# Diagonal blocks through memory at one stride, and two first sums placed behind the triangular steps, in a conformer and RWKV-7 trunk

## The chip, the cores and the metric

The kernel runs on one core of a Trainium2 chip. The metric is the device time of one execution in microseconds (us); smaller is better. All arithmetic is in 32-bit floating point; a product of large matrices is made of three matmuls on values split into a high and a low part (`xh·w_hi + xl·w_hi + xh·w_lo`).

## The reference

The program computes a decoder trunk of two layers on 512 tokens with 16 learned tokens ahead of them (528 in all), width 1024. A layer is a feed-forward half step, a token mixer and a second half step, each with a residual and a layer norm:

```python
h = _layer_norm(ALPHA * h + 0.5 * _swiglu(h, ffn1...), ...)
m = _mixer(h, ...)            # below
h = _layer_norm(ALPHA * h + m, ...)
h = _layer_norm(ALPHA * h + 0.5 * _swiglu(h, ffn2...), ...)

def _mixer(x, ...):
    z = x @ w_in
    glu_a, glu_b, zr, gate_c, gate_r = jnp.split(z, ...)
    yc = _conv_branch(glu_a, glu_b, ...)    # GLU, depthwise convolution of 31 taps, norm, silu, product
    yr = _rwkv_branch(zr, ...)              # 16 heads of 64
    return (sigmoid(gate_c) * yc + sigmoid(gate_r) * yr) @ w_out

def step(S, inp):                           # the recurrence of _rwkv_branch, per head, over tokens
    r_t, w_t, k_t, v_t, kk_t, a_t = inp
    sa = jnp.einsum("bhvk,bhk->bhv", S, -kk_t)
    S = S * w_t[:, :, None, :] + sa[..., None] * (kk_t * a_t)[:, :, None, :] \
        + v_t[..., None] * k_t[:, :, None, :]
    return S, jnp.einsum("bhvk,bhk->bhv", S, r_t)
```

After the recurrence each head's output gets a norm of its own (group norm), a bonus term and a gate.

## The kernel before, in words

The recurrence is computed in chunks: the 16 learned tokens, then eight chunks c = 0 to 7 of 64 tokens. Inside a chunk the steps are coupled by a lower triangular matrix of 64 x 64 for each head, which has to be inverted; between chunks only a 64 x 64 state is handed on. The 16 heads are worked through in four groups q = 0 to 3 of four heads. Of a group, these stages matter here:

- **Scores** (`scores`, L1354): for each chunk eight small matmuls on TensorE (PE) form the coupling matrix. ScalarE (ACT) copies it to `ut` (L1359), VectorE (DVE) masks the other parts (L1361, L1363), and SyncE (SP) writes it to a buffer in memory, `mscr<-ut` (L1366).
- **Substitution** (`substitution(q, g)`; g = 0 for chunks 0 to 3, g = 1 for chunks 4 to 7): a 64 x 64 matrix has four diagonal blocks of 16 x 16. They are loaded from memory so that each of 64 partitions holds one block, `im<-mscr` (L1380), inverted by 30 short DVE steps, the triangular steps (L1389 and L1392, `is<-im,ix` and `ix<-ix,is`), copied transposed by ACT (`it`, L1396), written to memory, `xdscr<-ix` and `xdscr<-it` (L1398), and read back into `dd`, `dd<-xdscr` (L1403), where the blocks stand on the diagonal of a 64 x 64 matrix whose other elements are zero. `dd` has two halves, f = 0 (from `ix`) and f = 1 (from `it`).
- **Inverse** (`inverse(q, g)`): PE completes the inverse of the whole matrices, first with half f = 0 (L1428), then with f = 1 (L1435), with a DVE operation after each step.
- **Scan**: chunk after chunk PE, ACT and DVE carry the state through (L1510, L1512, L1523, L1526, L1532, L1539). The inverse for g = 0 must be there before chunk 0, that for g = 1 before chunk 4.
- **Post**: group norm (`group_norm`; its first sum is `reduce_sum` at L1570, later `b<-b,gn_st` at L1585), bonus and gate of an earlier part, while the next group is under way.

The scan of one group overlaps scores and substitution of the next. At the last group, q = 3, there is no next group; there the convolution's norm begins: loads `G<-cscr` (L945) and seven additions on DVE over eight 128 x 528 pieces (L948, `conv_mean`), a sum over partitions on PE (L935), and `conv_norm` (L956 onward). The 31 taps of the convolution (L1183, `cacc`) run on DVE all through the mixer.

What keeps PE busy during these chains is a list of large products that don't depend on them: the gates' and GLU's share of `x @ w_in` (L250, matmuls of 128 x 264, below called fillers). They are handed out between the steps.

Each engine works in order. That order is chosen when the kernel is built, by a list scheduler with estimated durations of its own; it takes what is ready by its estimate, and obeys the dependences and order constraints without a semaphore (`nosync`), such as those between the triangular steps. So a change of a duration or of a constraint in one place may reorder all engines in the mixers.

Of the kernel before, what the change touches and what calls it, by code (L numbers as in the profile page):

```python
# [11 lines left out]
ALU = mybir.AluOpType  # L12
AX = mybir.AxisListType
# [3 lines left out]
P = 128  # L17
# [3 lines left out]
NM = 16  # L21
# [8 lines left out]
HS = 64  # L30
C = 64
NCH = SEQ // C
LN_EPS = 1e-5
GN_EPS = 64e-5
ALPHA = (2 * DEPTH) ** 0.25
# [72 lines left out]
class Trunk:  # L108
# [686 lines left out]
    def mixer(self, l, last, pre, more):  # L795
        nc, tc = self.nc, self.tc
        self.l, self.last = l, last
        self.t0, self.n = (NM, SEQ // 2) if last else (0, T // 2)
        dram = lambda name, shape: self.dp.tile(shape, F32, name=f"{name}{l}")
# [3 lines left out]
        self.gs = dram("gscr", [2 * D, T])  # L803
        self.us = dram("uscr", [D, T])
        self.ds, self.as_, self.ggs = dram("dscr", [D, T]), dram("ascr", [D, T]), dram("ggscr", [D, T])
        self.ms = dram("mscr", [4, NCH * 4, C, C])
        self.ms0 = dram("mscr0", [4, 4, NM, NM])
        self.xs0 = dram("xscr0", [4, 4, NM, NM])
        self.xd = dram("xdscr", [4, 2, 2, P // 2, NM, NM])
        ppool, self.pp = self.enter(f"mix_ps{l}", space=PSUM)  # L810
        pms = [self.mm() for _ in range(2)]
        self.glu0 = self.sc()
# [55 lines left out]
        N = prep(1)  # L868
        post = iter(())
        self.cuts = CUTS  # L870
        for q in range(4):
# [3 lines left out]
            for c, _ in enumerate(self.scan(q, Q)):  # L875
                if c == 0:
                    if q == 3:
                        self.tap_late = 150
                        self.taps(KT * TAPS)
                        cv = self.conv_mean()  # L880
# [58 lines left out]
    def conv_mean(self):  # L939
        nc, mp, t0, n = self.nc, self.mp, self.t0, self.n  # L940
        s = slice(t0, t0 + 2 * n)
        cv = self.rows().rearrange("p a b c t -> p (a b c) t")[:, :, s]
        csv = self.cs.rearrange("(o p) t -> p o t", p=P)
        for a, b in zip(CV, CV[1:]):
            nc.sync.dma_start(out=cv[:, a:b], in_=csv[:, a:b, s])  # L945
        ssum, mean = (mp.tile([P, T], F32, name="v", bufs=4)[:, 0:2 * n] for _ in range(2))
        for o in range(1, KT):
            nc.vector.tensor_tensor(ssum, cv[:, 0] if o == 1 else ssum, cv[:, o], op=ALU.add)  # L948
        nc.scalar.copy(mean.rearrange("p (h t) -> p h t", h=2), self.over_partitions(ssum))
        return cv, ssum, mean  # L950

# [110 lines left out]
    def mixer_begin(self, zs, filler):  # L1062
# [4 lines left out]
        z = self.tmp()  # L1067
# [72 lines left out]
            o += n  # L1140

        self.dd = mp.tile([P, NCH * 2, 2, C], F32, name="dd")
        nc.gpsimd.memset(self.dd, 0.0)


    def glu_b(self, ct):
# [162 lines left out]
    def scores(self, q, Q):  # L1309
# [30 lines left out]
        for c in range(NCH):  # L1340
            cs = slice(NM + c * C, NM + (c + 1) * C)
            fs = slice(2 * cs.start, 2 * cs.stop)
            ps = self.sc()
            for p in range(2):
                nc.tensor.transpose(ps[:, 0, 256 + p * P:256 + (p + 1) * P], FB[p][:, fs],
                                    self.ident)
            nc.scalar.copy(SB[:, c, :, C:2 * C],
                           ps[:, 0, 256:512].rearrange("p (h v) -> p h v", h=4))
            U = self.ut[C * (c % 2):C * (c % 2) + C, 4 * (c // 2):4 * (c // 2) + 4, :]
            pairs = []  # L1350
            for p in range(2):
                for e in range(2):
                    r = slice(HS * e, HS * e + HS)
                    pairs.append(nc.tensor.matmul(ps[:, e, p * P:(p + 1) * P], FB[p][r, fs],  # L1354
                                                  G[r, p, 1, :, cs], start=True, stop=True))
            for later, earlier in zip(pairs[1:], pairs):
                self.nosync(later, earlier)
            pv = ps[:, :, 0:2 * P].rearrange("a e (p f t) -> a e p f t", p=2, f=2)
            nc.scalar.copy(U.rearrange("a (p e) t -> a e p t", e=2), pv[C:P, :, :, 0, :])  # L1359
            mask = self.msk[:, :, None, None].to_broadcast([P, 2, 2, 2, C])  # L1360
            nc.vector.tensor_tensor(SB[:, c, :, 0:C].rearrange("a (p e) t -> a e p t", e=2),  # L1361
                                    pv[:, :, :, 1, :], mask[:, 1], op=ALU.mult)
            nc.vector.tensor_tensor(G[0:C, :, :, 0, cs].rearrange("a p e t -> a e p t"),  # L1363
                                    pv[0:C, :, :, 0, :], mask[0:C, 0], op=ALU.mult)
            to = 4 * (4 * (c // 4) + 2 * (c % 2) + c % 4 // 2)
            nc.sync.dma_start(out=self.ms[q, to:to + 4].rearrange("h j t -> j h t"), in_=U)  # L1366
            yield

    def substitution(self, q, g, Q):


        nc, mp, dd = self.nc, self.mp, self.dd
        N = NCH * 2
        blocks = [slice(NM * b, NM * b + NM) for b in range(4)]
        np_ = 4 * N + (4 if g == 0 else 0)
        M, X, XT = (mp.tile([P, NM, NM], F32, name=x, bufs=2)[0:np_] for x in ("im", "ix", "it"))
        nc.gpsimd.memset(X, 0.0)
        nc.gpsimd.memset(X.rearrange("s t i -> s (t i)")[:, 0::NM + 1], 1.0)
        for b, r in enumerate(blocks):
            nc.sync.dma_start(out=M[b * N:(b + 1) * N], in_=self.ms[q, g * N:(g + 1) * N, r, r])  # L1380
        if g == 0:
            nc.sync.dma_start(out=M[4 * N:], in_=self.ms0[q])
        steps = []
        for j in range(NM - 1):
            w, k = NM - 1 - j, j + 1
            y = mp.tile([P, 64], F32, name="is", bufs=2)[0:np_, 0:w * k]
            y = y.rearrange("s (t i) -> s t i", t=w)
            x = X[:, j + 1:, 0:k]
            steps.append(nc.vector.tensor_tensor(  # L1389
                y, M[:, j, j + 1:, None].to_broadcast([np_, w, k]),  # L1390
                X[:, j, None, 0:k].to_broadcast([np_, w, k]), op=ALU.mult))
            steps.append(nc.vector.tensor_tensor(x, x, y, op=ALU.add))  # L1392
        for later, earlier in zip(steps[1:], steps):
            self.nosync(later, earlier)
        self.hold = steps[-1]
        nc.scalar.copy(XT, X.rearrange("s t i -> s i t"))  # L1396
        for f, x in enumerate((X, XT)):
            nc.sync.dma_start(out=self.xd[q, g, f], in_=x[0:4 * N])  # L1398
            for b, r in enumerate(blocks):
                for e in range(2):  # L1400
                    o = C * e + NM * b
                    k = b * N + e * N // 2
                    nc.sync.dma_start(out=dd[o:o + NM, g * N // 2:(g + 1) * N // 2, f, r],  # L1403
                                      in_=self.xd[q, g, f, k:k + N // 2]
                                      .rearrange("s t i -> t s i"))
        if g == 0:
            nc.sync.dma_start(out=self.xs0[q], in_=XT[4 * N:])
            xt0 = mp.tile([P, 64], F32, name="xt", bufs=1)[0:NM].rearrange("a (s t) -> a s t", s=4)
            nc.sync.dma_start(out=xt0, in_=self.xs0[q].rearrange("s i t -> i s t"))
            Q["xt0"] = xt0  # L1410
# [150 lines left out]
    def group_norm(self, y, np_, m):  # L1561
# [5 lines left out]
        sq = mp.tile([P, NCH * 4, 32], F32, name="b4", bufs=B4)  # L1567
        sq = sq.rearrange("p a b -> p (a b)").rearrange("p (g v) -> p g v", v=HS)
        sb = st[:np_, :g, None].to_broadcast([np_, g, HS])
        nc.vector.reduce_sum(st[:np_, :g], yv, axis=AX.X)  # L1570
        if m in GNACT:
            mu = mp.tile([P, 16], F32, name="gn_mu", bufs=2)
            nc.vector.tensor_scalar_mul(mu, st, -1.0 / HS)
# [238 lines left out]
```

## Time and profile before

| | |
|---|---|
| time before, median of 3 runs (lowest to highest) | 3013.95 us (3011.65 to 3015.38) |
| the profiled execution: its time, its span | 3008.79 us, 3007.1 us |
| mean granted TensorE clock over the span | 0.994 |
| busy: PE, DVE, ACT, POOL | 2936.7, 2272.8, 1417.0, 181.4 us |
| TensorE not busy | 70.4 us |

The span runs from the first to the last instruction on the core. "PE" is TensorE's matmuls, "PEld" its weight loads, "SPq" a queue's own instructions on SyncE, which issue transfers. A wait is printed as engine, written tile and line, then what it waited for; then us in total, number of times, longest. The granted clock is 1.00 at full speed.

### The profile page before, as it was taken

What the parts mean: (1) busy time and instruction counts of PE and PEld (TensorE: products, weight loads), DVE (VectorE), ACT (ScalarE), POOL (GpSimd) and SP (SyncE); (2) the same over time, 40 slices, a digit from 0 to 9 for tenths busy, and PEclk for the clock granted to TensorE, in tenths of its full rate; (3) what the DMA queues carried; (4) which work ended last, traced back from release to release, by engine and by line L of the source; (5) the groups of instructions that cost most, each with busy time, mean ns of one, the idle gap of its engine ahead of it and who ended that gap; (6) DMA issues with size and microseconds to landing.
All of it is one profiled execution on the core that took longest, in us unless ns stands there. A gap on an engine that the chain in (4) does not pass through costs nothing. (4 is left out here: it accounts for less than half of the span.)

```text
span 3007.1 us, 64793 instructions
## 1 busy us (share of the span) xinstructions
PE 2936.7 (98%) x26420; PEld 2809.8 (93%) x26420; DVE 2272.8 (76%) x4657; ACT 1417.0 (47%) x2513; POOL 181.4 (6%) x288
## 2 busy tenths in 40 slices
PE   9999999999999999999999999999999989999998
PEld 8999989888888999999999999898888879999998
DVE  5776778998887768676776767789888777677767
ACT  4444444354555534444444444543444564355543
POOL 1110000000000000100001000000000000001100
PEclk9999999999999999999999999999999999999999
DMA  7565534435455645565555654444354656456651
GB/s 193 139 158 129 130 108 154 109 100 128 107 151 140 186 141 131 136 149 127 130 131 137 148 134 123 132 143 106 90 132 104 169 139 194 125 142 147 149 145 56
DMA packets 556152, 405.33 MB, mean 135 GB/s; under 512 B 89306, under 2 KB 500798, under 8 KB 555854
## 3 DMA queue, kind: packets, MB, share of 16 engines
q1 hardware_dynamic: 520302, 308.49, 36.0%
q0 software_dynamic: 30944, 84.18, 15.2%
q10 hardware_dynamic: 4608, 8.52, 0.8%
q8 instruction: 208, 3.41, 0.5%
q14 instruction: 90, 0.74, 0.1%
HBM read 270.81 MB, written 47.12 MB: 106 GB/s over the span
## 5 line engine op out<-in xcount | busy, mean ns | idle before, releaser
L218 PE MATMUL mm<-xh,w_hi 128*128 128x264 f32 (+1 forms) x1792 | 509.3, 286 | 13.0 <-ACT xh L463 8.7
L218 PE MATMUL mm<-xl,w_hi 128*128 128x264 f32 (+1 forms) x1792 | 509.4, 285 | 0.6 <-DVE xl L464 0.3
L218 PE MATMUL mm<-xh,w_lo 128*128 128x264 f32 (+1 forms) x1792 | 508.3, 284 | 0.0
L218 PE MATMUL mm<-hh,w_hi 128*128 128x264 f32 (+1 forms) x1408 | 399.6, 284 | 2.5 <-ACT hh L121 2.5
L218 PE MATMUL mm<-hh,w_lo 128*128 128x264 f32 (+1 forms) x1408 | 399.7, 284 | 0.0
L218 PE MATMUL mm<-hl,w_hi 128*128 128x264 f32 (+1 forms) x1408 | 399.3, 284 | 0.2
L250 PE MATMUL mm<-xh,w_hi 128*128 128x264 f32 x1760 | 387.2, 295 | 4.8 <-DVE tmp L1056 1.9
L250 PE MATMUL mm<-xl,w_hi 128*128 128x264 f32 x1760 | 379.8, 293 | 0.0
L1183 DVE SCALAR_TENSOR_TENSOR cacc<-cu,cw,cacc 128x528 f32<-128x528 f32 (+1 forms) x480 | 356.7, 753 | 3.6
L218 PEld LDWEIGHTS mm<-xh,w_hi 128*128 128x128 f32 x1792 | 336.6, 189 | 17.9 <-ACT xh L463 11.7
L218 PEld LDWEIGHTS mm<-xl,w_hi 128*128 128x128 f32 x1792 | 339.2, 189 | 2.9 <-DVE xl L464 2.4
L218 PEld LDWEIGHTS mm<-xh,w_lo 128*128 128x128 f32 x1792 | 338.8, 189 | 0.1
L131 ACT CAST w_hi<-sums 128x512 fp32r<-128x512 f32 (+1 forms) x204 | 154.6, 759 | 313.0 <-PE mm L218 201.7
L250 PEld LDWEIGHTS mm<-xh,w_hi 128*128 128x128 f32 x1760 | 279.4, 190 | 14.9 <-DVE tmp L1056 2.3
L250 PEld LDWEIGHTS mm<-xl,w_hi 128*128 128x128 f32 x1760 | 278.1, 190 | 7.2 <-issue 0.2
L218 PEld LDWEIGHTS mm<-hh,w_hi 128*128 128x128 f32 x1408 | 264.7, 188 | 3.1 <-ACT hh L121 2.9
L218 PEld LDWEIGHTS mm<-hl,w_hi 128*128 128x128 f32 x1408 | 264.9, 188 | 0.9 <-DVE hl L122 0.8
L218 PEld LDWEIGHTS mm<-hh,w_lo 128*128 128x128 f32 x1408 | 265.4, 189 | 0.1
L250 PE MATMUL mm<-xh,w_lo 128*128 128x264 f32 x1760 | 262.1, 292 | 0.0
L155 ACT CAST w_hi<-w_raw 128x1024 fp32r<-128x1024 f32 x130 | 136.2, 1050 | 257.3 <-PE mm L218 77.6
L164 DVE TENSOR_TENSOR w_lo<-w_raw,w_hi 128x1024 fp32r<-128x1024 f32 (+1 forms) x194 | 201.5, 1042 | 64.2 <-ACT w_hi L155 60.3
L250 PEld LDWEIGHTS mm<-xh,w_lo 128*128 128x128 f32 x1760 | 229.6, 189 | 6.4
(375 smaller groups left out, 6672.0 us busy)
## 6 DMA issues: line engine op xcount, KB each, us to landing
w_raw<-in_w_in_dram SPq DMA_DIRECT2D x116, 512.0 KB
w_lo<-w_raw POOLq DMA_DIRECT2D x100, 512.0 KB, 5.1
w_raw<-in_ffn_wg_dram SPq DMA_DIRECT2D x88, 512.0 KB
w_raw<-in_ffn_wu_dram SPq DMA_DIRECT2D x88, 512.0 KB
w_raw<-in_ffn_wd_dram SPq DMA_DIRECT2D x80, 512.0 KB
w_lo<-w_raw POOLq DMA_DIRECT2D x68, 256.0 KB, 3.6
w_raw<-in_conv_wo_dram SPq DMA_DIRECT2D x16, 512.0 KB
w_raw<-in_rwkv_wo_dram SPq DMA_DIRECT2D x16, 512.0 KB
```

The source lines that it names most:

```text
L131: self.nc.scalar.copy(hi, x)
L155: copy = self.nc.scalar.copy(hi[:, :kt], raw[:, :kt])
L164: sub = self.nc.vector.tensor_tensor(lo[:, k], raw[:, k], hi[:, k].bitcast(F32), op=ALU.subtract)
L218: self.issued = self.nc.tensor.matmul(pm, a[:, k, :], b[:, xk + k, s], start=first and k == 0 and j == 0, stop=last and k == nk - 1 and j ...
L250: m = self.issued = self.nc.tensor.matmul(pm[:, h, :n], a[:, wk + k, :], b[:, xk + k, s:s + n], start=first and i == 0, stop=last and i == ...
L1183: tap = nc.vector.scalar_tensor_tensor(y, x, w, y, op0=ALU.mult, op1=ALU.add)
```

## The change

- Each row of `mscr` (one 64 x 64 matrix) gets 64 words of room behind it, so that a row has 4160 = 4 x 1040 words. The diagonal blocks start 16 x 64 + 16 = 1040 words apart, so all 16 x 16 blocks of all rows lie at one stride. `im<-mscr` becomes one transfer of 64 x 16 x 16 elements in place of four of 16 x 16 x 16.
- `xdscr` becomes one buffer for both layers and all groups, with rows of 4160 words, zeroed once in layer 0 by two transfers of 512 KB on GpSimd's queue. `xdscr<-ix` and `xdscr<-it` write the blocks to their places on the diagonals: 1024 pieces of 64 bytes each, where they were 64 rows of 1 KB. `dd<-xdscr` then reads whole 64 x 64 matrices, zeros included: four transfers of 64 x 8 x 64 (two for each half f, pieces of 256 bytes) in place of sixteen of 16 x 8 x 16 (pieces of 64 bytes).
- `dd` is set to zero by GpSimd (L1143) in layer 0 alone.
- The first sum of group norm (L1570) and the additions of `conv_mean` (L948) get a `nosync` constraint: they come, in DVE's order, behind the last triangular step that has been put into the program so far (`self.solved`).

```diff
+DIAG = NM * (C + 1)
...
-        self.ms = dram("mscr", [4, NCH * 4, C, C])
+        self.ms = dram("mscr", [4, NCH * 4, 4 * DIAG])
...
-        self.xd = dram("xdscr", [4, 2, 2, P // 2, NM, NM])
+        if l == 0:
+            self.xd = dram("xdscr", [2, 2, NCH * 2, 4 * DIAG])
...
         for o in range(1, KT):
-            nc.vector.tensor_tensor(ssum, cv[:, 0] if o == 1 else ssum, cv[:, o], op=ALU.add)
+            add = nc.vector.tensor_tensor(ssum, cv[:, 0] if o == 1 else ssum, cv[:, o],
+                                          op=ALU.add)
+            self.nosync(add, self.solved)
...
-        nc.gpsimd.memset(self.dd, 0.0)
+        if self.l == 0:
+            nc.gpsimd.memset(self.dd, 0.0)
+            zero = self.dd.rearrange("p s f i -> p (s f i)")
+            xd = self.xd.rearrange("g f r z -> (g f r) z")
+            for a in range(2):
+                nc.gpsimd.dma_start(out=xd[:, a * C * C // 2:(a + 1) * C * C // 2],
+                                    in_=zero[a * C:(a + 1) * C])
...
+    def diagonal(x):
+
+        x = x.rearrange("r (b z) -> (r b) z", b=4)[:, 0:NM * C]
+        return x.rearrange("p (t i) -> p t i", i=C)[:, :, 0:NM]
...
-        for b, r in enumerate(blocks):
-            nc.sync.dma_start(out=M[b * N:(b + 1) * N], in_=self.ms[q, g * N:(g + 1) * N, r, r])
+        nc.sync.dma_start(out=M[0:4 * N], in_=self.diagonal(self.ms[q, g * N:(g + 1) * N]))
...
-        self.hold = steps[-1]
+        self.hold = self.solved = steps[-1]
         nc.scalar.copy(XT, X.rearrange("s t i -> s i t"))
         for f, x in enumerate((X, XT)):
-            nc.sync.dma_start(out=self.xd[q, g, f], in_=x[0:4 * N])
-            for b, r in enumerate(blocks):
-                for e in range(2):
-                    o = C * e + NM * b
-                    k = b * N + e * N // 2
-                    nc.sync.dma_start(out=dd[o:o + NM, g * N // 2:(g + 1) * N // 2, f, r],
-                                      in_=self.xd[q, g, f, k:k + N // 2]
-                                      .rearrange("s t i -> t s i"))
+            nc.sync.dma_start(out=self.diagonal(self.xd[g, f]), in_=x[0:4 * N])
+        for f in range(2):
+            rows = self.xd[g, f, :, 0:C * C].rearrange("(e s) (t i) -> e t s i", e=2, i=C)
+            for e in range(2):
+                nc.sync.dma_start(out=dd[C * e:C * e + C, g * N // 2:(g + 1) * N // 2, f],
+                                  in_=rows[e])
...
-        nc.vector.reduce_sum(st[:np_, :g], yv, axis=AX.X)
+        self.nosync(nc.vector.reduce_sum(st[:np_, :g], yv, axis=AX.X), self.solved)
```

The lines of the changed kernel stand 1 to 13 lines lower, so L1366 became L1376, L1380 L1395, L1389 and L1392 L1404 and L1407, L1398 L1413, L1403 L1417, L1428 L1441.

The scheduler moves instructions on every engine. Three places show how.

SP in mixer 1 at q = 3, before: from the write of the coupling matrices of chunk 7 (`mscr<-ut`) to the reading of `dd`.

```order
L1366 DMA mscr_22952<-ut 64x4x64
L1638 DMA bon<-bscr_22946 128x256
L1380 DMA im<-mscr_22952 16x16x16 x3
L1398 DMA xdscr_22955<-ix 64x256
L1380 DMA im<-mscr_22952 16x16x16
L1398 DMA xdscr_22955<-it 64x256
L1407 DMA xscr_22954<-it 4x256
L1403 DMA dd<-xdscr_22955 16x8x16 x16
```

The same place on SP after; `G<-cscr` are the loads for the convolution's norm, which stood ahead of the last two `mscr<-ut` before.

```order
L947 DMA G<-cscr_22827 128x4x512
L1376 DMA mscr_22834<-ut 64x4x64
L947 DMA G<-cscr_22827 128x3x512
L1413 DMA xdscr_4680<-ix 64x16x16
L1413 DMA xdscr_4680<-it 64x16x16
L1420 DMA xscr_22836<-it 4x256
L1376 DMA mscr_22834<-ut 64x4x64
L1417 DMA dd<-xdscr_4680 64x8x64 x4
L1422 DMA xt<-xscr_22836 16x4x16
L1395 DMA im<-mscr_22834 64x16x16
```

The results of g = 0 (`xdscr<-ix`) went from behind the blocks of g = 1 (`im<-mscr`) to ahead of the last `mscr<-ut`, and the loads of `dd` stand ahead of `im<-mscr` for g = 1.

DVE at the same place before: the last triangular steps of g = 0 (`is<-im,ix`, `ix<-ix,is`) with the masks of chunk 7 (L1361, L1363) and the convolution norm's additions (L948) between them.

```order
L1585 TENSOR_TENSOR b_28683<-b_28683,gn_st 128x1024
L1389 TENSOR_TENSOR is<-im,ix 68x63
L948 TENSOR_TENSOR v<-G 128x512
L1392 TENSOR_TENSOR ix<-ix,is 68x7x9
L948 TENSOR_TENSOR v<-v,G 128x512
L1389 TENSOR_TENSOR is<-im,ix 68x60
L1361 TENSOR_TENSOR sb<-sc,msk 128x2x2x64
L1392 TENSOR_TENSOR ix<-ix,is 68x6x10
L1363 TENSOR_TENSOR G<-sc,msk 64x2x2x64
L1389 TENSOR_TENSOR is<-im,ix 68x55
L948 TENSOR_TENSOR v<-v,G 128x512
L1392 TENSOR_TENSOR ix<-ix,is 68x5x11
```

After, the first masks in this stretch are those of chunk 6 and the last ones those of chunk 7.

```order
L1407 TENSOR_TENSOR ix<-ix,is 68x7x9
L1404 TENSOR_TENSOR is<-im,ix 68x60
L1371 TENSOR_TENSOR sb<-sc,msk 128x2x2x64
L1407 TENSOR_TENSOR ix<-ix,is 68x6x10
L1373 TENSOR_TENSOR G<-sc,msk 64x2x2x64
...
L1404 TENSOR_TENSOR is<-im,ix 68x15
L1407 TENSOR_TENSOR ix<-ix,is 68x15
L1193 SCALAR_TENSOR_TENSOR cacc<-cu_23088,cw,cacc 128x512 x3
L1371 TENSOR_TENSOR sb<-sc,msk 128x2x2x64
L1193 SCALAR_TENSOR_TENSOR cacc<-cu_23088,cw,cacc 128x512
L1373 TENSOR_TENSOR G<-sc,msk 64x2x2x64
L1193 SCALAR_TENSOR_TENSOR cacc<-cu_23088,cw,cacc 128x512 x10
```

The additions and the group norm's large operations are gone from among the steps, and the steps end ahead of the masks of chunk 7.

PE at the same place, from the last scores (L1354) to the first matmul of the inverse (L1428). The rows of L250 are fillers, and x16 means sixteen in a row. Before, there are 111 of them in this stretch, and two transposes (L1501).

```order
L1354 MATMUL sc<-G,FB 128x128 x4
...
L250 MATMUL mm<-xh,w_lo 128x264 x16
L1501 MATMUL tr<-ident,v 128x128 x2
L250 MATMUL mm<-xh,w_hi 128x264 x2
...
L250 MATMUL mm<-xh,w_hi 128x264
L1428 MATMUL sc<-dd,ut 64x64
```

After, the stretch has 63 fillers; it begins and ends as follows.

```order
L1364 MATMUL sc<-G,FB 128x128 x4
L251 MATMUL mm<-xl,w_hi 128x264 x2
...
L251 MATMUL mm<-xh,w_lo 128x264 x16
...
L251 MATMUL mm<-xh,w_hi 128x264
L1441 MATMUL sc<-dd,ut 64x64
```

The first inverse moved forward by 48 fillers there, which are now handed out later, among the steps of the scan. In the eight groups (q = 0 to 3 of mixer 0, then of mixer 1) the number of fillers between the last score and the first inverse is 125, 125, 99, 138, 136, 106, 98, 111 before, and 88, 68, 49, 61, 92, 42, 49, 63 after.

More of the change, by code (lines that the diff above doesn't have):

```diff
@@ L1365, in scores @@
             to = 4 * (4 * (c // 4) + 2 * (c % 2) + c % 4 // 2)
-            nc.sync.dma_start(out=self.ms[q, to:to + 4].rearrange("h j t -> j h t"), in_=U)
+            nc.sync.dma_start(out=self.ms[q, to:to + 4, 0:C * C]
+                              .rearrange("h (j t) -> j h t", t=C), in_=U)
             yield
+    @staticmethod
+    def diagonal(x):
+        x = x.rearrange("r (b z) -> (r b) z", b=4)[:, 0:NM * C]
+        return x.rearrange("p (t i) -> p t i", i=C)[:, :, 0:NM]
     def substitution(self, q, g, Q):
@@ L1373, in substitution @@
         N = NCH * 2
-        blocks = [slice(NM * b, NM * b + NM) for b in range(4)]
         np_ = 4 * N + (4 if g == 0 else 0)
```

## The prediction

> **What bounds the kernel now.** I read the page's head first, then TensorE's waits, then stretches of time around the waits that the change can reach.
>
> ```profile
> span 3007.1 us, 64793 instructions
> PE 2936.7 (98%) x26420; PEld 2809.8 (93%) x26420; DVE 2272.8 (76%) x4657; ACT 1417.0 (47%) x2513; POOL 181.4 (6%) x288
> ```
>
> TensorE is busy for all but 70 us of the span. Nothing in the change takes a matmul away, so it can only win what PE waits, and what PE loses in speed after waiting. The waits of PE (us in total, times, longest) that belong to the mixers:
>
> ```profile
> PE ch L1523 <- ACT w L1512: 9.1, 6, 4.5
> PE tr L1510 <- ACT va L1505: 8.7, 5, 3.7
> PE sc L1428 <- DMA dd<-xdscr: 6.9, 3, 4.7
> PE sc L1435 <- DMA dd<-xdscr: 3.6, 3, 2.8
> ```
>
> The two last rows are waits for the blocks that the change transports: 10.5 us. Nearly all of it is three events, at q = 3 of either mixer; I call these the two ends:
>
> ```profile
> 918.73 0.30 PE L1428 MATMUL sc<-dd,ut 64*64 64x64 f32 x2 [2.01 <-DMA dd<-xdscr]
> 927.74 0.29 PE L1435 MATMUL sc<-dd,b 64*64 64x64 f32 x2 [2.83 <-DMA dd<-xdscr]
> 2411.39 0.45 PE L1428 MATMUL sc<-dd,ut 64*64 64x64 f32 x2 [4.74 <-DMA dd<-xdscr]
> ```
>
> Next the stretches behind them (start and end, length, then busy us of PE, PEld, DVE, ACT, POOL; the third number from the right is the granted clock):
>
> ```profile
> 919.50:923.00 3.50, 3.50 (x38) 3.37 (x38) 3.50 (x10) 0.24 (x1) 0.84 (x1) 0.52 1.10 232
> 929.70:936.50 6.80, 6.80 (x64) 6.02 (x62) 3.24 (x11) 0.58 (x2) 0.00 (x0) 0.50 0.33 108
> 2411.10:2417.90 6.80, 6.51 (x50) 6.07 (x51) 5.54 (x15) 0.00 (x0) 0.00 (x0) 0.50 0.40 91
> ```
>
> The clock is at half (0.52, 0.50, 0.50) for 3.5, 6.8 and 6.8 us. PE counts as busy there and does half the work, so a second price hangs on each of these waits: 1.7 + 3.4 + 3.4 = 8.5 us. With the waits, 2.0 + 2.8 + 4.7 = 9.5, the two ends cost **18 us**.
>
> [...]
>
> **Why the blocks are late.** The chain of waits at the second end (start, us, what):
>
> ```profile
> 2393.52 6.67 DMA mscr<-ut
> 2401.64 5.09 DMA xdscr<-ix
> 2407.14 0.43 SPq L1403
> 2409.51 1.78 DMA dd<-xdscr
> ```
>
> `xdscr<-ix` starts at 2401.64, though the triangular steps of g = 0 end at 2398.85:
>
> ```profile
> 2390.43 0.41 DVE L1363 TENSOR_TENSOR G<-sc,msk 64x256 f32<-64x256 f32 x1
> 2391.15 1.21 DVE L1585 TENSOR_TENSOR b<-b,gn_st 128x1024 f32<-128x1024 f32 x1
> 2391.95 0.72 PE L1354 MATMUL sc<-G,FB 64*128 64x128 f32 x8
> 2397.58 0.19 DVE L1389 TENSOR_TENSOR is<-im,ix 68x39 f32<-68x39 f32 x1
> 2398.68 0.17 DVE L1392 TENSOR_TENSOR ix<-ix,is 68x15 f32<-68x15 f32 x1
> ```
>
> SP stood at `im<-mscr` of g = 1, which waits for the last `mscr<-ut` to land (6.67 us). Then eight loads for f = 0 are issued, about 0.45 us apart, and the last lands 1.78 us later. From the last score (2391.95, call it T) to the inverse it takes 19.4 us.
>
> **The change, part by part.**
>
> (a) *Issues of `dd`.* For f = 0 eight become two: 6 x 0.45 = 2.7 us less ahead of L1428; for f = 1 the same again. Where SP is held up, one row prices all sixteen:
>
> ```profile
> 906.96 2.57 SPq L1380 DMA_DIRECT2D im<-mscr  x4
> 910.37 0.67 SPq L1398 DMA_DIRECT2D xdscr<-ix  x1
> 914.03 9.95 SPq L1403 DMA_DIRECT2D dd<-xdscr  x16
> ```
>
> That is 0.62 us each at the first end, and its f = 1 loads came so late that L1435 waited its 2.83 us: 12 issues less are 7.5 us there, so that wait should go even where L1428 comes some us earlier.
>
> (b) *Order on SP.* `xdscr<-ix` stands ahead of the last `mscr<-ut`, and `im` for g = 1 behind `dd`. The wait for `mscr<-ut` leaves this chain: 2401.64 - 2398.85 less one issue, some 2.3 us. What is late next is `im` for g = 1; the blocks of g = 1 are needed at chunk 4 only, which PE reached 32 us after the first inverse:
>
> ```profile
> 2443.70 0.33 PE L1428 MATMUL sc<-dd,ut 64*64 64x64 f32 x2
> ```
>
> (c) *Order on DVE.* The additions of L948 and group norm's first operations leave the triangular steps:
>
> ```profile
> L948 DVE TENSOR_TENSOR v<-v,G x12: 674/692/698, 900.5 to 2437.8; 128x528 f32<-128x528 f32 x6, 128x512 f32<-128x512 f32 x6
> L1570 DVE TENSOR_REDUCE gn_st<-b x10: 629/1205/1220, 668.8 to 2486.8; 128x16 f32<-128x1024 f32 x6, 128x8 f32<-128x512 f32 x4
> ```
>
> Six additions at 0.69 us are 4.1 us; the sum over 1024 elements is 1.2 us, and L1585 behind it 1.2 again. The steps themselves are about 0.22 us apart (2397.58 to 2398.68 in five spacings). In the changed order two steps of g = 0 stand between the masks of chunk 6 (the second of which starts at 2390.43, T - 1.5) and eight more behind: 10 x 0.22 us, so that they end near T + 1, where it was T + 6.9. The displaced additions come after the steps of g = 1, and the convolution's norm with them. It has cover: DVE waited 6.0 us at its last addition for a load, and PE has over 100 fillers between there and the end of the scan.
>
> ```profile
> DVE v L948 <- DMA G<-cscr: 6.0, 1, 6.0
> ```
>
> (d) *PE's order gives part of it back.* The scheduler moved each first inverse forward. A filler's price:
>
> ```profile
> 2285.76 12.15 PE mm L250 x98
> ```
>
> 0.124 us. At the second end 111 fillers became 63: PE is there at T + 0.7 + 7.8 = T + 8.5. Now the chain: steps end at T + 1.0, issue 0.6, `xdscr<-ix` as slow as it was (5.1), two issues 0.9, landing 1.8: T + 9.4, a wait of about 1. With 3.7 us, as at the first end (910.37 to 914.03), it is T + 8.0 and no wait. So the order was drawn tight: the 10 us by which the blocks come sooner are nearly all spent on PE coming sooner, and what stays is the wait's size, not the shift. At q = 0 to 2, where PE hardly waits now, the same happens: 125, 125, 99 and 136, 106, 98 fillers become 88, 68, 49 and 92, 42, 49. The tightest is q = 1 of mixer 1: PE is there at T + 0.7 + 42 x 0.124 = T + 5.9, and its steps end four behind the masks of chunk 6, about T + 0. With a landing of 2.3 the blocks come at T + 5.6.
>
> (e) *The price of the new `xdscr` write* appears nowhere: 1024 pieces of 64 bytes to memory. Lower bound: 2.0 us, issue to release of the reader, where 64 rows of 1 KB meet little traffic. Upper bound: 6.7, the landing of `mscr<-ut` above. The nearest are the loads `im<-mscr`, which have the same pieces: 4.1 us from the fourth issue (2402.91) to DVE's next step (2407.00).
>
> ```profile
> 677.63 0.48 SPq L1398 DMA_DIRECT2D xdscr<-ix  x1
> 679.64 8.63 SPq L1403 DMA_DIRECT2D dd<-xdscr  x16
> 2402.91 0.58 SPq L1380 DMA_DIRECT2D im<-mscr  x1
> 2407.00 0.17 DVE L1389 TENSOR_TENSOR is<-im,ix 64x15 f32<-64x15 f32 x1 [4.35 <-DMA im<-mscr]
> ```
>
> I take 4 us. Then six of the eight groups get waits between 0 and 2 us, where before they had none. I put 0.7 us on each of the eight (5.6 us). Half clock behind them I leave out, since the shortest of the three waits above that had it behind it is 2.01 us. Rounded, **6 us** in all; bounds 0 and 26 (eight times 1.5, and half clock worth 1.7 behind each).
>
> [...]
>
> (f) *The rest.* One `dd` memset of GpSimd in layer 1 goes, and two transfers of 512 KB come in layer 0:
>
> ```profile
> w_raw<-in_w_in_dram SPq DMA_DIRECT2D x116, 512.0 KB
> ```
>
> That is the size of two of these weight loads among 116. POOL is busy for 6% of the span, so I put nothing on either. `im` as one transfer saves SP the 1.4 us of the three first issues at the second end; that lies in (b).
>
> **The sum.** 3008.8 (the profiled execution) - 18 + 6 = 2996.8 us. The median of the runs lies 5.2 us above the profiled one, so 3002 us.
>
> **The rivals.**
>
> *More goes.* TensorE's first wait above, for `w`, has ACT standing at another transfer:
>
> ```profile
> 733.75 0.83 ACT L1275 ACTIVATE k<-a,omka,half 128x528 f32<-128x528 f32 x1 [3.43 <-DMA a<-ascr]
> 735.38 0.37 PE L1523 MATMUL ch<-w,G 64*64 64x64 f32 x1 [4.53 <-ACT w L1512]
> 2232.92 0.68 PE L1510 MATMUL tr<-sv,G 128*64 128x64 f32 x8 [3.67 <-ACT va L1505]
> 735.40:742.00 6.60, 6.60 (x64) 5.79 (x65) 2.37 (x5) 3.86 (x7) 0.85 (x1) 0.50 0.81 216
> 2233.60:2237.00 3.40, 3.40 (x27) 2.57 (x26) 0.00 (x0) 1.49 (x5) 0.85 (x1) 0.50 0.59 116
> ```
>
> With waits of 4.5 and 3.7 us and half clock worth 3.3 and 1.7, these two places cost 13 us. SP issues `a<-ascr` behind the sixteen `dd` of g = 1, so it may come earlier by 12 x 0.45 = 5 us. Against it: this `k` still stands ahead of `w` on ACT after, and the load still stands behind weight loads on SP. If they go: 2989.
>
> *The time comes back.* The tight order (d) turns the two ends' waits into as many small ones, with half clock behind some, or fewer fillers between the last scan steps leave PE waiting there. The 18 us are then lost again: 3014, no change.
>
> *Slower.* The 64-byte write lands late: not 4 us after its issue but 6 to 6.7, the upper bound. Each of the eight chains then waits 0.7 + 2.0 to 0.7 + 2.7 us, eight times 2.7 to 3.4 is 22 to 27 us, and the waits of this size above had half clock behind them, worth 1.7 each time, 14 us more: 36 to 41, less the 18: 3032 to 3037. It decides from a landing of about 5.3 us, where eight waits of 2.0 us take up most of the gain.
>
> **How the numbers follow.** The likeliest case has 0.46; more goes, 0.10; it comes back, 0.26; slower, 0.18. What a measurement of this kernel can tell from no change is about 0.2%, 6 us: faster is below 3008, slower above 3020. The likeliest case's own range is 2994 to 3010 (6 us of new waits, between 0 and 14), so 0.42 of it is faster; with 0.10 of the first rival and 0.07 of the second (parts of the waits stay gone) that makes 0.59. Same: 0.04 + 0.17 + 0.02 = 0.23. Slower: 0.16 of the last rival and 0.02 of the one before, 0.18. The range leaves out half of the first rival and most of the last: 2987 to 3025.
>
> **What the profile will show.** The two rows of waits for `dd<-xdscr` shorter than 5 us together, spread over more groups; full clock in the stretches at both ends; `xdscr<-ix` issued within 3 us of the last score at q = 3; from its issue to the first `dd` issue about 4 us; the wait at L948 for `G<-cscr` gone. The forecast is wrong if that landing is over 6 us, if half clock shows behind more than two group ends, or if PE's waits for ACT or DVE in the scan at q = 3 grow by over 5 us.

## The result and the profile after

The changed kernel takes 2993.22 us (median of 4 runs, 2989.16 to 2996.34) against 3014.66 us before: ratio 0.993, 95% interval 0.9917 to 0.9944, that is 17 to 25 us less. Forecast were 12 us less.

The profiled execution took 2996.34 us, the slowest of the four. The page's head, then the waits of TensorE that answer to those shown of before (us in total, times, longest):

```profile
span 2994.6 us, 64362 instructions
PE 2937.3 (98%) x26420; PEld 2813.1 (94%) x26420; DVE 2278.5 (76%) x4657; ACT 1417.9 (47%) x2513; POOL 181.2 (6%) x289
```

```profile
PE tr L1523 <- DVE sv L1552: 5.8, 11, 2.4
PE sc L1261 <- ACT tmp L1259: 4.0, 4, 2.2
PE sc L1441 <- DMA dd<-xdscr: 2.6, 3, 2.0
PE tr L1523 <- ACT va L1518: 2.5, 2, 1.3
PE ch L1536 <- ACT w L1525: 1.8, 3, 0.9
```

PE's busy time is the same; PE not busy fell from 70.4 to 57.3 us. The waits for `dd` fell from 10.5 to 2.6 us, and those of the scan for ACT (`w`, `va`) from 17.8 to 4.3. New or longer are a wait for `tmp` on ACT and one of the scan for DVE. The longest for `tmp` (2.23 us at 730) has ACT standing 2.21 us at a load of the convolution, `cu<-uscr`, in the operation ahead of it. DVE's wait of 6.0 us at L948 for `G<-cscr` is gone, as forecast. The waits for `dd`, and the longest of all in the mixers (start, us, what, in brackets the wait ahead of it):

```profile
681.91 0.29 PE L1441 MATMUL sc<-dd,ut 64*64 64x64 f32 x2 [0.47 <-DMA dd<-xdscr]
907.75 0.29 PE L1441 MATMUL sc<-dd,ut 64*64 64x64 f32 x2 [1.97 <-DMA dd<-xdscr]
2061.68 0.32 PE L1441 MATMUL sc<-dd,ut 64*64 64x64 f32 x2 [0.17 <-DMA dd<-xdscr]
2377.11 1.08 PE L1523 MATMUL tr<-sv,G 128*64 128x64 f32 x8 [2.45 <-DVE sv L1552]
```

At the end of mixer 0 a wait of 1.97 us is left where there were 2.01 and 2.83; at the end of mixer 1 none, where there were 4.74. The stretches around both ends (start and end, length, busy of PE, PEld, DVE, ACT, POOL; third from the right the granted clock):

```profile
905.50:908.00 2.50, 0.53 (x6) 0.28 (x4) 2.39 (x4) 0.06 (x1) 0.84 (x1) 1.00 1.07 268
908.00:911.50 3.50, 3.50 (x38) 3.26 (x39) 1.11 (x2) 0.00 (x0) 0.00 (x0) 0.63 1.06 179
2376.50:2383.30 6.80, 6.19 (x46) 5.41 (x46) 4.39 (x20) 2.42 (x7) 0.00 (x0) 0.51 0.32 75
2383.30:2386.80 3.50, 3.50 (x18) 2.77 (x19) 2.17 (x10) 1.28 (x4) 0.00 (x0) 0.50 0.85 281
2386.80:2398.00 11.20, 11.16 (x91) 10.57 (x91) 10.05 (x18) 5.72 (x10) 1.69 (x2) 1.00 0.90 214
```

Half clock is still there: one stretch behind the 1.97 us, and some 10 us of it from within the new wait of 2.45 us that ends at 2377. The last row holds the first inverse of mixer 1's end, at 2396.89, at full clock.

That new wait is on DVE. Three of its operations there, in order:

```profile
2375.25 0.17 DVE L1404 TENSOR_TENSOR is<-im,ix 68x15 f32<-68x15 f32 x1 [2.09 <-DMA im<-mscr]
2375.45 0.43 DVE L1551 TENSOR_TENSOR sv<-ch,sv 64x256 f32<-64x256 f32 x1
2376.54 0.42 DVE L1552 TENSOR_TENSOR sv<-sv,pc 64x256 f32<-64x256 f32 x1
```

The first triangular step of g = 0 waits 2.09 us for its blocks to land, and the scan's `sv` stands behind it in DVE's order, so PE waits too.

I measured the two mixers in each profile, from the first gate product to the first product of the mixer's output, and added up within them PE's waits and the time lost to half clock (stretches below 0.95, length times the missing share). Us, both mixers together; the medians and ratios are of the timed runs.

| kernel | median | ratio to before (95%) | fillers ahead of the first inverses, 8 groups | mixers | PE waits | of these for `dd` | half clock |
|---|---|---|---|---|---|---|---|
| before | 3014.66 | 1 | 125 125 99 138 136 106 98 111 | 1155.0 | 38.8 | 10.5 | 13.6 |
| changed | 2993.22 | 0.9930 (0.9917 to 0.9944) | 88 68 49 61 92 42 49 63 | 1134.8 | 23.2 | 2.6 | 11.9 |
| changed, again | 2992.05 | 0.9927 (0.9909 to 0.9946) | the same | 1127.0 | 22.1 | 3.6 | 5.1 |
| transfers alone | 3005.39 | 0.9979 (0.9965 to 0.9992) | 88 92 87 95 92 63 87 69 | 1145.5 | 32.7 | 7.9 | 13.6 |
| order alone | 3007.05 | 0.9975 (0.9965 to 0.9985) | 125 102 57 71 136 102 63 70 | 1143.9 | 35.5 | 11.9 | 13.6 |
| sixteen loads | 3001.82 | 0.9963 (0.9951 to 0.9975) | 99 58 54 72 106 88 59 71 | 1144.4 | 30.4 | 5.7 | 10.2 |
| no conv order | 3004.87 | 0.9969 (0.9960 to 0.9978) | 88 68 49 61 92 42 49 63 | 1153.3 | 34.8 | 6.5 | 17.0 |
| no group norm order | 2996.70 | 0.9942 (0.9926 to 0.9958) | 88 92 87 71 92 63 87 54 | 1139.8 | 25.1 | 9.3 | 10.2 |
| late conv loads | 2994.39 | 0.9935 (0.9920 to 0.9951) | 88 68 49 51 92 42 49 54 | 1131.4 | 25.6 | 5.0 | 5.1 |
| four `im` | 2992.16 | 0.9921 (0.9906 to 0.9936) | 111 74 64 63 121 88 53 61 | 1132.4 | 22.9 | 6.2 | 13.6 |
| four `im`, late conv loads | 2998.01 | 0.9951 (0.9936 to 0.9965) | 111 74 64 61 121 88 53 64 | 1137.5 | 27.3 | 9.3 | 13.6 |

A profile is one execution: the two of the changed kernel have the same order of instructions, and their mixers differ by 7.8 us, of which 6.8 are half clock. Differences of a few us between two rows of the right-hand columns say little; the ratios rest on more runs.

Between before and the changed kernel the mixers got 20.2 us shorter: 15.6 of waits, 1.7 of half clock; the other 3 us I could not place in the waits that the profile prints.

### The profile page after: what moved, and what is told of

Its sections match the earlier page's. It is cut to its first block, busy times and chain, and to the rows that moved or that the text cites. A ratio compares the mean times of both kernels' runs of the same rounds, so it can differ in the third digit from the quotient of the medians.

```text
span 2994.6 us, 64362 instructions
## 1 busy us (share of the span) xinstructions
PE 2937.3 (98%) x26420; PEld 2813.1 (94%) x26420; DVE 2278.5 (76%) x4657; ACT 1417.9 (47%) x2513; POOL 181.2 (6%) x289
## 5 line engine op out<-in xcount | busy, mean ns | idle before, releaser
L219 PE MATMUL mm<-xh,w_hi 128*128 128x264 f32 (+1 forms) x1792 | 510.4, 287 | 13.6 <-ACT xh L464 9.8
L219 PE MATMUL mm<-xl,w_hi 128*128 128x264 f32 (+1 forms) x1792 | 510.6, 285 | 0.6 <-DVE xl L465 0.3
L219 PE MATMUL mm<-xh,w_lo 128*128 128x264 f32 (+1 forms) x1792 | 509.8, 285 | 0.0
L219 PE MATMUL mm<-hh,w_hi 128*128 128x264 f32 (+1 forms) x1408 | 400.3, 285 | 2.4 <-ACT hh L122 2.4
L219 PE MATMUL mm<-hh,w_lo 128*128 128x264 f32 (+1 forms) x1408 | 400.5, 285 | 0.0
L219 PE MATMUL mm<-hl,w_hi 128*128 128x264 f32 (+1 forms) x1408 | 400.1, 284 | 0.2
L219 PEld LDWEIGHTS mm<-xh,w_hi 128*128 128x128 f32 x1792 | 337.9, 189 | 18.1 <-ACT xh L464 12.8
L219 PEld LDWEIGHTS mm<-xl,w_hi 128*128 128x128 f32 x1792 | 340.5, 190 | 2.9 <-DVE xl L465 2.4
L219 PEld LDWEIGHTS mm<-xh,w_lo 128*128 128x128 f32 x1792 | 340.2, 190 | 0.1
L219 PEld LDWEIGHTS mm<-hh,w_hi 128*128 128x128 f32 x1408 | 265.5, 189 | 2.9 <-ACT hh L122 2.6
L219 PEld LDWEIGHTS mm<-hl,w_hi 128*128 128x128 f32 x1408 | 265.7, 189 | 0.9 <-DVE hl L123 0.8
L219 PEld LDWEIGHTS mm<-hh,w_lo 128*128 128x128 f32 x1408 | 266.2, 189 | 0.1
```

The lines of the kernel that those rows point to most:

```text
L219: self.issued = self.nc.tensor.matmul(pm, a[:, k, :], b[:, xk + k, s], start=first and k == 0 and j == 0, stop=last and k == nk - 1 and j ...
```

## The experiments

**The two halves of the change apart.** Transfers alone: the changed kernel without the two `nosync` lines.

```diff
-        self.nosync(nc.vector.reduce_sum(st[:np_, :g], yv, axis=AX.X), self.solved)
+        nc.vector.reduce_sum(st[:np_, :g], yv, axis=AX.X)
-            self.nosync(add, self.solved)
```

> The change's transfers (one im load, diagonal xdscr write, four dd loads), without the two order constraints on DVE. Theory A (both halves are needed, since the blocks come sooner through fewer issues and through earlier triangular steps): about half of the gain of 21 us, 3004 us, with waits for dd at L1441 of 3 to 6 us at the two q=3 ends. Theory B (order alone): no gain, 3014. Theory C (transfers alone): all of it, 2993.

Order alone: the kernel before with these lines put in.

> The kernel before with the two order constraints alone; four im loads, packed xdscr, sixteen dd loads. Theory A: about half, 3004 us; the sixteen issues keep the blocks 3 to 5 us late at the q=3 ends, since the first inverse moved forward there too (138 to 71 and 111 to 70 fillers). Theory B: 2993. Theory C: 3014.

Measured: 9 us less than the kernel before it (3014.28 beside these runs) for the transfers alone, 7 us for the order alone (by the ratios 6 and 8). Each is less than half of 21 us; theory A holds, B and C fall. Their longest waits at PE, first of the transfers alone, then of the order alone:

```profile
916.82 0.44 PE L1440 MATMUL sc<-dd,ut 64*64 64x64 f32 x2 [6.29 <-DMA dd<-xdscr]
```

```profile
912.08 0.44 PE L1430 MATMUL sc<-dd,ut 64*64 64x64 f32 x2 [5.26 <-DMA dd<-xdscr]
2405.63 0.44 PE L1430 MATMUL sc<-dd,ut 64*64 64x64 f32 x2 [4.20 <-DMA dd<-xdscr]
```

Both wait longer at the end of mixer 0 than the kernel before did in its two waits there (2.01 and 2.83 us): the scheduler moved the inverse forward in both, to 95 and 71 fillers from 138, and the blocks did not come that much sooner. SyncE's queue shows what held them: of the transfers alone, then of the order alone (start, us for the issues, what, number).

```profile
905.16 0.60 SPq L1394 DMA_DIRECT2D im<-mscr  x1
906.61 0.70 SPq L1412 DMA_DIRECT2D xdscr<-ix  x1
913.70 3.35 SPq L1416 DMA_DIRECT2D dd<-xdscr  x4
```

```profile
898.00 0.48 SPq L1400 DMA_DIRECT2D xdscr<-ix  x1
905.61 9.14 SPq L1405 DMA_DIRECT2D dd<-xdscr  x16
```

Without the order the steps end late, at 903.6, SP then stands at `im<-mscr`, and `xdscr<-ix` is issued at 906.61. Without the transfers it is issued at 898.00, but sixteen loads take 9.14 us to issue, and the first inverse needs eight of them. The changed kernel has both early:

```profile
898.32 0.59 SPq L1413 DMA_DIRECT2D xdscr<-ix  x1
902.39 6.60 SPq L1417 DMA_DIRECT2D dd<-xdscr  x4
```

A third difference lies between these rows: from the write to the first `dd` it takes 7.1 and 7.6 us in the two halves, with SP waiting for the write to land in the second (it issued nothing from 900.41 to 905.61), and 4.1 in the changed kernel. That is 3 us of the difference at this end, and the rows don't show which part of the edits sets it; at the end of mixer 1 the three are nearer, 4.6, 5.8 and 5.6 us.

**Which transfer.** The changed kernel with the packed `xdscr`, one for each layer, and sixteen loads of `dd` as before, `dd` being set to zero in both layers; the one `im` load and the order stay. The blocks come from `im` in another sequence than these loads assume, so they land in other places of `dd`; shapes and counts of all transfers are as said.

```diff
-            nc.sync.dma_start(out=self.diagonal(self.xd[g, f]), in_=x[0:4 * N])
-        for f in range(2):
-            rows = self.xd[g, f, :, 0:C * C].rearrange("(e s) (t i) -> e t s i", e=2, i=C)
-            ...
+            nc.sync.dma_start(out=self.xd[q, g, f], in_=x[0:4 * N])
+            for b, r in enumerate(blocks):
+                for e in range(2):
+                    ...
```

> The changed kernel with the packed xdscr write (64 rows of 1 KB) and the sixteen dd loads of before; the one im load and the order constraints stay. Theory A: im matters little, so the same as order alone, 3004 us. Theory B: 2993. Theory C with im as the part that counts: 2993, with dd as the part that counts: 3014. If the 64-byte writes cost time, some of it is won back here: xdscr to dd issue shorter by 1 to 2 us.

And the changed kernel with four loads `im`:

```diff
-        nc.sync.dma_start(out=M[0:4 * N], in_=self.diagonal(self.ms[q, g * N:(g + 1) * N]))
+        m = self.ms[q, g * N:(g + 1) * N].rearrange("r (b z) -> b r z", b=4)[:, :, 0:NM * C]
+        for b in range(4):
+            nc.sync.dma_start(out=M[b:4 * N:4],
+                              in_=m[b].rearrange("r (t i) -> r t i", i=C)[:, :, 0:NM])
```

> The changed kernel with four loads im<-mscr of 16x16x16 in place of one; everything else stays. Three SP issues more (3 x 0.45 us) on the way of the triangular steps. Theory A (im matters little, at most its issues): 0 to 5 us slower than the changed kernel, 2993 to 2998. Rival (the one load is a large part, since the steps of g=0 end sooner by it): 3001 or more.

Sixteen loads: 3001.82, some 9 us of the gain lost (ratio 0.9963 against 0.9930, intervals apart). Four `im`: 2992.16, no loss at all (intervals overlap). So of the transfers it is `dd` that counts, and the single load of `im` brought nothing that shows in the time. But the sixteen loads cost little through the waits for `dd`, 5.7 us in all. The longest wait of PE in that kernel, 3.63 us, comes from another load that stood behind them on SP, `a<-ascr`, for which ACT waited 8.62 us:

```profile
2308.45 8.31 SPq L1412 DMA_DIRECT2D dd<-xdscr  x16
2318.03 0.70 SPq L1231 DMA_DIRECT2D a<-ascr  x1
2325.84 0.83 ACT L1278 ACTIVATE k<-a,omka,half 128x528 f32<-128x528 f32 x1 [8.62 <-DMA a<-ascr]
2327.83 0.68 PE L1519 MATMUL tr<-sv,G 128*64 128x64 f32 x8 [3.63 <-ACT va L1514]
```

The price of the new write shows on SP. In the changed kernel and in the one before, where SP really stood waiting ahead of the first `dd`, from the issue of `xdscr<-ix` to that `dd`:

```profile
2416.50 0.60 SPq L1413 DMA_DIRECT2D xdscr<-ix  x1
2419.04 2.75 SPq L1417 DMA_DIRECT2D dd<-xdscr  x4
```

```profile
702.61 0.45 SPq L1398 DMA_DIRECT2D xdscr<-ix  x1
704.60 7.44 SPq L1403 DMA_DIRECT2D dd<-xdscr  x16
```

2.54 us with 1024 pieces of 64 bytes, 1.99 with 64 rows of 1 KB. The shortest of all such pairs are 2.53 to 2.56 us in every kernel with the small pieces, and 1.93 to 1.96 in every one without. The write costs 0.6 us more, and 12 issues less at 0.45 to 0.6 us pay for it several times. The longest are 7.1 us with the pieces and 7.6 with the rows of 1 KB, so either form varies by 5 us, and the forms differ by 0.6.

**Which constraint.** The changed kernel without the one on the convolution norm's additions, and without the one on group norm's first sum (a line each, as in the first diff).

> The changed kernel without the constraint on the convolution norm's additions; group norm's stays. Fillers ahead of each first inverse are the same as in the changed kernel. Theory A: the additions (7 x 0.69 us) may stand among the steps of g=0 at the two ends again, so the blocks come up to 4 us later there: 4 to 8 us slower than the changed kernel, 2997 to 3001, with the wait at L1441 grown at q=3. Rival: the scheduler puts them elsewhere anyway: 2993.

> The changed kernel without the constraint on group norm's first sum; the one on the convolution norm's additions stays. Fillers ahead of the first inverses: 88, 92, 87, 71, 92, 63, 87, 54, so at q=1 and 2 the first inverse comes as late as with the transfers alone. Theory A (each constraint acts where its sums stand: conv at the two ends, group norm at q=1, 2 and behind): between the transfers alone (3005) and the changed kernel (2993), near 3000, with the waits for dd at the ends as short as in the changed kernel. Rival (the conv constraint alone carries the order's gain): 2993. Rival (group norm's carries it): 3005.

Without the conv constraint 3004.87: 12 us slower than the changed kernel, more than theory A's 4 to 8 allowed. Its first wait at the ends, then that without group norm's constraint:

```profile
904.42 0.30 PE L1440 MATMUL sc<-dd,ut 64*64 64x64 f32 x2 [3.39 <-DMA dd<-xdscr]
```

```profile
908.26 0.45 PE L1441 MATMUL sc<-dd,ut 64*64 64x64 f32 x2 [4.72 <-DMA dd<-xdscr]
2390.43 0.44 PE L1441 MATMUL sc<-dd,ut 64*64 64x64 f32 x2 [2.97 <-DMA dd<-xdscr]
```

Without group norm's, 2996.70: 3 to 4 us slower, with intervals that overlap the changed kernel's, although the waits for `dd` are 9.3 us in all. The expectation that the waits at the ends stay short there failed. So the conv constraint carries most of the order's gain in time, and not through the waits for `dd` alone: without it they are 6.5 us, but the scan waits longer for ACT:

```profile
PE ch L1535 <- ACT w L1524: 7.9, 4, 3.5
```

In the changed kernel this row has 1.8 us. Two waits make up most of it, one in the last scan steps of either mixer, and the trace shows what ACT stood at: a weight load of the convolution's output product, whose conversion comes ahead of `w` on ACT.

```profile
974.31 1.14 ACT L154 CAST w_hi<-w_raw 128x512 fp32r<-128x512 f32 x2 [2.86 <-DMA w_raw<-in_conv_wo_dram]
975.77 0.37 PE L1535 MATMUL ch<-w,G 64*64 64x64 f32 x1 [3.45 <-ACT w L1524]
2470.57 0.62 ACT L154 CAST w_hi<-w_raw 128x512 fp32r<-128x512 f32 x1 [3.21 <-DMA w_raw<-in_conv_wo_dram]
2471.51 0.27 PE L1535 MATMUL ch<-w,G 64*64 64x64 f32 x1 [3.54 <-ACT w L1524]
```

With 5.1 us of half clock around these 7.0 us of waits they are as large as the 12 us. In the changed kernel no operation of ACT waits for that weight. The triangular steps, theory A's reason, hardly moved: at the two ends they finish 1.4 and 0.5 us behind the start of the last score, against 0.8 behind and 0.8 ahead of it in the changed kernel, and 3.2 and 0.8 behind it without group norm's constraint.

**What is left at the ends.** The changed kernel with the convolution norm's loads ordered behind `dd` on SP.

```diff
-            nc.sync.dma_start(out=cv[:, a:b], in_=csv[:, a:b, s])
+            self.nosync(nc.sync.dma_start(out=cv[:, a:b], in_=csv[:, a:b, s]), self.read0)
```

> The changed kernel with one more constraint on SP: the loads G<-cscr for the convolution's norm come behind the four dd loads of g=0. In the changed kernel 1.75 MB of them are issued within 6 us ahead of xdscr<-ix at q=3, whose landing took 4.1 and 5.6 us there against 2.5 to 2.8 elsewhere, and four dd issues took 6.6 us. Theory (traffic of G<-cscr is what delays the blocks at the ends): landing 2.6 to 3 us at both ends, dd issues 2.6 us, wait at L1441 in mixer 0 (1.97 us) under 0.7; time 2 to 4 us less, 2989 to 2991. Rival (the loads come too late for the convolution's norm): a wait at L937 or L948 of 3 us or more and 2995 or above.

```profile
906.85 0.30 PE L1443 MATMUL sc<-dd,ut 64*64 64x64 f32 x2 [3.38 <-DMA dd<-xdscr]
897.21 0.57 SPq L1413 DMA_DIRECT2D xdscr<-ix  x1
900.43 7.76 SPq L1417 DMA_DIRECT2D dd<-xdscr  x4
```

SP came to the first `dd` sooner, 3.2 us behind the write for 4.1. (Those 4.1 us were not the landing, as the expectation reads them: in the changed kernel SP was issuing other transfers until 0.09 us ahead of that `dd`.) But the four `dd` took 7.76 us to issue where 2.6 were expected and 6.60 measured in the changed kernel, and the inverse was still late: 2994.39, the same as the changed kernel. The wait grew from 1.97 to 3.38 us; 1.2 us of that is the scheduler's, which moved the inverse forward by another 10 fillers of 0.124 us (51 for 61). The theory that the loads' traffic is the price falls, and no wait for the late loads showed either. What stretches the `dd` issues there stays open.

Last, both variants together, beside the changed kernel once more:

> The changed kernel once more, unchanged, beside the next kernel on one chip, so that differences of 2 to 5 us between variants can be judged: 2990 to 2996 us, ratio to before 0.992 to 0.994; the waits for dd at L1441 2 to 4 us in all.

> The changed kernel with four im loads and with the loads G<-cscr behind dd on SP. Theory (im is neutral, and the conv loads' traffic costs 2 to 4 us at the two ends): 2988 to 2991 and 2 to 4 us less than the changed kernel beside it. Rival (whatever comes sooner at the ends is spent by the order of PE, as the single variants showed): the same as the changed kernel within 3 us.

2992.05 and 2998.01: two edits that cost nothing alone cost 6 us together, with intervals that just overlap; neither the theory nor the rival for the second came. With them the first inverse of mixer 0's end waits longest:

```profile
909.58 0.44 PE L1446 MATMUL sc<-dd,ut 64*64 64x64 f32 x2 [4.85 <-DMA dd<-xdscr]
```

No version beat the changed kernel beyond its interval.

## Why the prediction was right, and where it was off

Direction and mechanism held; 21 us were measured for 12 forecast, inside the range. That the total came so near is in part luck: some terms that were not in the sum are as large as those that were, and partly cancel (see the end of this section).

- **The 18 us at the two ends.** Waits of 9.5 us became 2.0, half clock of 8.5 became 1.7: 14.3 us less instead of 18, in one execution. How much half clock hangs on a wait differs between executions (11.9 and 5.1 us in the mixers of the two profiles; last section). The reading that waits of about 2 us drag half clock behind them was confirmed by this trace: a clock of 0.50 for 3.41 us behind the wait of 1.97, and for 10.24 us from within the wait of 2.45. "Half the work" was a little too dear: at 0.50 the matmuls of L219 start 0.22 us apart (366.39 to 369.47), behind that stretch 0.12 (369.67 to 372.95).
- **(a) and (b), the issues and the order on SP.** Right, and both needed: the kernels with one half of the change alone won 9 and 7 us. "`im` as one transfer" was rightly put at next to nothing.
- **(c), the order on DVE.** The steps end as early as worked out: with T = 897.44 and 2388.27, the working put the issue of `xdscr<-ix` at T + 1.6; it came at 898.32, 0.7 us sooner than that, and at 2387.51, 2.4 us sooner. What the step missed is how much hangs on the conv constraint, 12 us, and why: without it the steps still end early, but ACT stands at the convolution's weights in the last scan steps. The steps' early end at the first end is group norm's constraint more than the additions'.
- **(d), PE's order gives part of it back.** Right, and the most useful step. At the second end PE was forecast at T + 8.5 and the first inverse came at T + 8.6, without a wait. The variants show it: blocks that come sooner are met by an inverse that the scheduler put sooner.
- **(e), the price of the write, the term that was mis-sized.** Taken at 4 us from the loads `im<-mscr` with the same pieces. From the issue to the first `dd` of g = 0 it took 2.7 to 3.0 us at six groups, and 4.1 and 5.6 at the two ends, where SP was issuing other transfers until 0.09 us ahead of that `dd`; the least is 2.5. So 5.6 us of new waits at the eight groups turned out as 2.6 us, 1.97 of them at one end that had had 4.84. What made the nearest row longer, the profile of before doesn't show. That the 2.0 us were taken in "little traffic" doesn't hold: the DMA engines were busy for 0.67 of the stretch of those loads (2402.91 to 2407.00, 140 GB/s), and for 0.61 and 0.67 of two where a write of 64 rows took 2.0 us (677.60 to 680.00 and 702.60 to 704.60, 161 and 179 GB/s). (The likeliest case's own range is also off by a little: new waits of 0 to 14 us give 2996 to 3010, not 2994.) The 64-byte pieces cost 0.6 us a write. The fourth case, which needed a landing of 5.3 us at eight groups, did not come: only one of the eight reached that distance.
- **The first rival, "more goes", was given 0.10, and its number largely came, its mechanism not.** The two places priced at 13 us (waits of 4.53 and 3.67 and half clock of 3.4 and 1.7) have 2.23 and 1.32 + 0.51 of waits and one half-clock stretch of 1.7 after: 5.8, or 7.5 us less. The argument against it, that `k` still stands ahead of `w` on ACT, looked at rows of the order without asking when they run. But `a<-ascr` did not come earlier, as the rival said: at the first place it was issued at 725.83 before and at 736.78 after, and there `k` follows at 742.29 without a wait. It is the order that did it and not the shorter `dd` on SP: the same sum is 10.4 us with the transfers alone and 5.9 with the order alone. With the transfers alone ACT still waits for `a` at the first place, and PE for ACT:

```profile
734.64 0.83 ACT L1284 ACTIVATE k<-a,omka,half 128x528 f32<-128x528 f32 x1 [3.65 <-DMA a<-ascr]
736.77 1.12 PE L1522 MATMUL tr<-sv,G 128*64 128x64 f32 x8 [3.04 <-ACT va L1517]
```

- **What was not on the list**: the scan's `sv` behind a triangular step that waits for `im`, 2.45 us and 5.1 us of half clock in one execution. In the second profile of the changed kernel the same place hardly waits, so its price is not steady:

```profile
2371.38 0.65 PE L1523 MATMUL tr<-sv,G 128*64 128x64 f32 x8 [0.27 <-DVE sv L1552]
```

Term by term, in the mixers: -14.3 at the ends, -0.3 for waits for `dd` elsewhere (0.9 before, 0.6 after) and -7.5 at the first rival's places. Against them stand +7.6 at 2377 and +3.4 of half clock at 2093, around a wait of 1.69 us for DVE. Smaller waits elsewhere are 6 us less, 2.5 of it one wait for `w` at 2436 in the kernel before. The 3 us that lie in no printed wait make up the rest of -20.2. So the two terms of the sum, -18 and +6, came as -14.3 and -0.3, and the rest stood in neither. Outside the mixers this execution lost 12 us to half clock and the one of before 4, in stretches that no part of the change touches; that is why its span fell by 12.5 us only, less than the mixers and less than the medians.

## What to carry to other kernels

Where an in-order engine is fed through a chain of transfers and a scheduler fills the gap with other work, look at how far it moves the consumer forward when the chain gets shorter: the wait that stays is the difference of the two, and halves of an edit can each make it longer. Count issues on the queue before bytes or piece sizes: twelve issues less, at 0.45 to 0.6 us each, won what a write in 1024 small pieces hardly cost (0.6 us). And price small waits with the half clock behind them, but from several executions, since the same order of instructions showed 5 and 12 us of it.

## What the runs showed of the hardware that was not expected

A write of 64 KB to memory in 1024 pieces of 64 bytes took 2.53 to 2.56 us at least from issue to the next dependent issue, against 1.93 to 1.96 us for 64 rows of 1 KB: 0.6 us in all. Two profiled executions of the changed kernel, the same program, lost 24.0 and 10.6 us to half clock over the whole span and had spans of 2994.6 and 2983.8 us, so half clock covers the difference. It does not follow from a wait's length alone: in the first of the two, this wait at the border of a feed-forward part has a half-clock stretch behind it (366 to 370),

```profile
365.62 0.39 PE L219 MATMUL mm<-hh,w_hi 128*128 128x264 f32 x1 [2.36 <-ACT hh L122]
```

while in the kernel before, nearly the same wait at the same place has full clock behind it:

```profile
364.15 0.39 PE L218 MATMUL mm<-hh,w_hi 128*128 128x264 f32 x1 [2.29 <-ACT hh L121]
```

What differs is where the wait falls. In each of the eleven profiles all half-clock stretches begin whole multiples of 3.413 us apart and, but for one cut off by the end of the span, last whole multiples of it: in the first profile of the changed kernel six last 3.413 us, two 6.827 and one 10.240, in the kernel before four last 3.413 us and three 6.827, and in both the beginnings fit steps of 3.4133 us to within 0.001 us. So in these profiles they lie on a grid of such steps, and its position is another in each execution (first beginnings at 11.22 and 11.52 us). The wait of 2.36 us lies within one step, that of 2.29 us on two. The steps in question and those behind them, first with half clock and then without (columns as above):

```profile
362.80:366.21 3.41, 0.97 (x6) 0.55 (x6) 3.27 (x7) 0.96 (x3) 0.00 (x0) 1.00 0.49 143
366.21:369.62 3.41, 3.41 (x16) 3.41 (x17) 2.43 (x5) 2.61 (x3) 0.00 (x0) 0.50 0.63 167
359.68:363.10 3.42, 2.18 (x19) 1.97 (x17) 2.49 (x3) 1.85 (x2) 0.00 (x0) 1.00 0.04 8
363.10:366.51 3.41, 2.28 (x16) 2.08 (x17) 2.79 (x8) 1.88 (x4) 0.00 (x0) 1.00 1.00 264
366.51:369.92 3.41, 3.41 (x31) 3.41 (x30) 2.97 (x6) 1.83 (x3) 0.00 (x0) 1.00 0.42 93
```

In the first PE is idle for 2.4 of 3.4 us; in the third and fourth for 1.2 and 1.1. In the first profile of the changed kernel and that of before (without the first 20 and the last 12 us of the span) ten steps at full clock had PE idle for 1.9 us or more, and behind all ten came half clock; of 1689 with less than 1.1 us it came behind none, of the 19 between behind four. Over all eleven profiles my counts are 47 of 47, three of 9299 and 30 of 108. So in these profiles a wait of some 2 us had half clock behind it where nearly all of it fell within one step, less often where two steps shared it, and one profile's half clock is not the kernel's.
